# Four PSUM banks for each pool throughout, the first z tile's projection moved ahead, the final norm's sums on TensorE

## The chip, the cores and the metric

The kernel runs on one core of a Trainium2 chip. The metric is the device time of one execution in microseconds. The engines are TensorE (PE, with its weight loads shown as PEld), VectorE (DVE), ScalarE (ACT), GpSimd (POOL) and SyncE (SP), which only issues transfers. TensorE writes to PSUM, of which there are eight banks of 512 float32 values in each of 128 partitions; VectorE and ScalarE read it from there.

## The reference

One layer of an encoder for 384 tokens (128 of running streams, 256 of a new one), all in float32. Cut to what matters:

```
h    = rmsnorm(x, norm1_w);  proj = h @ w_in       # z, x/B/C, dt, u, v
xbc  = silu(causal_conv(x/B/C))
dt   = softplus(dt_raw + dt_bias)
y    = ssd_scan(xs, dt, a, B, C, h0) + d * xs       # 8 groups of 4 heads
y    = group_rmsnorm(y * silu(z))
g    = gelu(u) * spatial_mix(group_rmsnorm(gelu(v)))
x    = x + concat(y, g) @ w_out
h    = rmsnorm(x, norm2_w);  up = causal_conv(h @ w_up)
x    = x + (silu(up[:D_FF]) * up[D_FF:]) @ w_down
out  = x * rsqrt(mean(x * x) + EPS) * final_norm_w
```

The outputs are `out`, the new states of the convolutions and of the scan, and the normalised `v` rows of the running streams.

## The kernel before

Activations lie transposed: 16 tiles `xT` of 128 features by 384 tokens. Every large product is made of three reduced-precision (fp32r) matmuls. Both operands are split into a high part (a cast on ScalarE) and a low part (a subtraction on VectorE): `hh` and `hl` for the normed input, `whi` and `wlo` for a slab of weights. `mm3` (L95 to L97) issues high by high, high by low, low by high. A slab (`slab`, L82) is 128 x 1024 weights; it is loaded by SP into `wraw`, split, and read by 24 matmuls. The pool `wpool` has three buffers for each of `wraw`, `whi` and `wlo`.

`in_proj` (L201) makes one tile of 128 projected features: two slabs, 48 matmuls of 384 columns, in one PSUM bank. The factor 1/rms of a norm is multiplied in afterwards, when VectorE reads the bank.

The order: the first block loads `xT`, sums its squares into `ssum1` and makes the first four tiles of group 0 (`ps_first`) and the `dt` product (`ps_dt`). `rstd_of` (L99) then sums `ssum1` over the partitions with a matmul (L103), takes a root on ScalarE and a reciprocal on VectorE (L111): `r1`. Three transposes of `r1` (L198) give `r1t`, six small records (L255) rearrange `dt`, and a chain of short VectorE instructions makes `dt`, its running sums (L285 to L287) and the decays.

Eight groups of heads follow: `ssd_in(g)` makes the six tiles Bc, Cc, xs0, xs1, zs0, zs1; `ssd(g)` does the scan, with small matmuls between VectorE and ScalarE work (transposes L362 and L371, products L392 to L414, `dk` times `xdt` L456, the new state L488, the group norm L107). The last group's `ssd` is followed by `gmlp(0)`, whose first part `gmlp_v` (L528 to L530) multiplies weights `w_v` as the moving operand, 512 columns, into three banks `pv` at once. Then come three more `gmlp` calls with `w_out` between them, the second norm, and the feed-forward part, `up` and `down`, in eleven chunks. At the end, squares of `xT` are summed into `ssum3` on GpSimd, the last on VectorE; a matmul with one column (L672) sums over partitions; `rt` is the reciprocal root; `rd` is a diagonal of it, and a float32 matmul (L678) spreads it over the partitions; 16 products (L680) give the output.

PSUM is handed out by two pools, `psA` (projections) and `psB` (all else): 3 and 5 banks for the heads. Behind the heads both are closed and opened anew as 4 and 4 (L510 to L512). A tile of a pool waits until a bank of that pool is free. The new pools lie on the banks of the old ones.

The order of each engine's instructions is fixed before the run by a planner: it takes the instruction that is ready in its own timeline and comes first in the program; `tc.high_priority` (the first block and all slabs) moves instructions ahead. On the chip each engine keeps that order.

Of the kernel before, what the change touches and what calls it, by code (L numbers as in the profile page):

```python
# [9 lines left out]
F32 = mybir.dt.float32  # L10
F32R = mybir.dt.float32r
BF16 = mybir.dt.bfloat16
AF = mybir.ActivationFunctionType
ALU = mybir.AluOpType
PSUM = bass.MemoryType.PSUM

P = 128
D = 2048
KT = D // P
NB, LS, LP = 8, 16, 256  # L20
T = NB * LS + LP
NT = T // P
# [15 lines left out]
def encoder_layer(ctx: ExitStack, tc: tile.TileContext, a: dict, o: dict):  # L38
    nc = tc.nc

    def mul(out, x, y, eng=None):
        (eng or nc.vector).tensor_tensor(out=out, in0=x, in1=y, op=ALU.mult)  # L42

    def add(out, x, y, eng=None):
        (eng or nc.vector).tensor_tensor(out=out, in0=x, in1=y, op=ALU.add)  # L45

    def sub(out, x, y, eng=None):
        (eng or nc.vector).tensor_tensor(out=out, in0=x, in1=y, op=ALU.subtract)  # L48
# [4 lines left out]
    def act(out, x, f, **kw):  # L53
        nc.scalar.activation(out=out, in_=x, func=f, **kw)

    const = ctx.enter_context(tc.tile_pool(name="const", bufs=1))
    wpool = ctx.enter_context(tc.tile_pool(name="wpool", bufs=3))
    mixp = ctx.enter_context(tc.tile_pool(name="mixp", bufs=3))
    big = ctx.enter_context(tc.tile_pool(name="big", bufs=1))
    ps_ctx = ExitStack()  # L60
    psA = ps_ctx.enter_context(tc.tile_pool(name="psA", bufs=3, space=PSUM))
    psB = ps_ctx.enter_context(tc.tile_pool(name="psB", bufs=5, space=PSUM))
    dram = ctx.enter_context(tc.tile_pool(name="dram", bufs=1, space=bass.MemoryType.DRAM))

    def ctile(name, shape, src=None, eng=None):
# [6 lines left out]
    xT = [big.tile([P, T], F32, name=f"xT{k}") for k in range(KT)]  # L72
# [26 lines left out]
    def rstd_of(ssum, n, name, pool, parts=None):  # L99

        ps = psB.tile([P, 512], F32, name="psb")
        if parts is None:
            nc.tensor.matmul(ps[:, :T], ones, ssum, start=True, stop=True)  # L103
        else:
            split(ssum, *parts)
            for i, x in enumerate(parts):
                nc.tensor.matmul(ps[:, :T], onesr, x, start=i == 0, stop=i == 1)  # L107
        sq = pool.tile([P, T], F32, name=name + "_q", tag="rsq")
        act(sq, ps[:, :T], AF.Sqrt, bias=eps, scale=1.0 / n)
        r = pool.tile([P, T], F32, name=name, tag="rstd")  # L110
        nc.vector.reciprocal(out=r, in_=sq)  # L111
        return r
# [19 lines left out]
    ssum1 = const.tile([P, T], F32, name="ssum1", tag="ssum")  # L132
    first_ctx = ExitStack()
    fst_p = first_ctx.enter_context(tc.tile_pool(name="first", bufs=1))
    ps_dt = psB.tile([P, 512], F32, name="psb")
    ps_first = [(psB if j == 3 else psA).tile([P, 512], F32, name="psb" if j == 3 else "psa") for j in range(4)]
    with tc.high_priority(offset=AHEAD):
        warm = fst_p.tile([P, 512], BF16, name="warm")
        nc.vector.memset(warm, 0.0)
# [36 lines left out]
        ones = ctile("ones", [P, P], eng=nc.sync)  # L176
        ident = ctile("ident", [P, P], eng=nc.sync)
# [12 lines left out]
    nfw = ctile("final", [P, KT])  # L190
    onesr = const.tile([P, P], F32R, name="onesr")
    nc.vector.tensor_copy(out=onesr, in_=ones)
    r1 = rstd_of(ssum1, D, "r1", const)
    first_ctx.close()
    r1t = const.tile([P, NT], F32, name="r1t")
    psr = psB.tile([P, 512], F32, name="psb")
    for t in range(NT):
        nc.tensor.transpose(out=psr[:, t * P : (t + 1) * P], in_=r1[:, t * P : (t + 1) * P], identity=ident)  # L198
    nc.scalar.copy(out=r1t, in_=psr[:, : NT * P].rearrange("p (t i) -> p t i", t=NT)[:, :, 0])

    def in_proj(src, ps=None):  # L201

        ps = psA.tile([P, 512], F32, name="psa") if ps is None else ps
        for half in range(2):
            hi, lo = slab(src[half])
            for k in range(8):
                kk = half * 8 + k
                mm3(ps[:, :T], w_of((hi, lo), k), (hh[kk], hl[kk]), kk == 0, kk == KT - 1)
        return ps

    def w_out(cs, mixes, done=None):

# [44 lines left out]
    x, e, s, q, p = (m2[:, i * W : (i + 1) * W] for i in range(5))  # L257
# [78 lines left out]
    def ssd_in(g):  # L336
        cst = sp.tile([P, 4, NB + 1, KC - 1], F32, name="cst", bufs=2)
        nc.gpsimd.dma_start(out=cst, in_=a["conv_st"][g])
        nst = sp.tile([P, 4, NB + 1, KC - 1], F32, name="nst", bufs=2)
        h0 = sp.tile([P, NB, 4 * HD], F32, name="h0")  # L340
        nc.gpsimd.dma_start(out=h0, in_=a["h0T"][g])
        res = []
        for j, nm in enumerate(("Bc", "Cc", "xs0", "xs1")):
            ps = ps_first[j] if g == 0 else in_proj(a["w_ssd"][g, j])
            t = sp.tile([P, T], F32, name=nm, bufs=2)
            conv_silu(ps, 4 * g + j, cst, nst, j, t)
            res.append(t)
        nc.gpsimd.dma_start(out=o["nconv"][g], in_=nst)
        for j in range(2):
            ps = in_proj(a["w_ssd"][g, 4 + j], psB.tile([P, 512], F32, name="psb") if g == j == 0 else None)  # L350
            t = sp.tile([P, T], F32, name=f"zs{j}")
            mul(t, ps[:, :T], r1)
            act(t, t, AF.Silu)
            res.append(t)
        return res + [h0]

    def ssd(g, Bc, Cc, xs0, xs1, zs0, zs1, h0):
# [123 lines left out]
        Bh = sp.tile([P, P], F32R, name="Bh")  # L481
        Bl = sp.tile([P, P], F32R, name="Bl")
        split(Bt[:, 0], Bh, Bl)
        pn = [psB.tile([P, 512], F32, name="psb") for _ in range(NB // 2)]
        for i, (w, x) in enumerate(((Bh, xwh), (Bh, xwl), (Bl, xwh))):
            for q in range(NB // 2):
                rows = slice(32 * q, 32 * q + 32)
# [19 lines left out]
            w_out([g // 2 - 1], [mixes[g - 2], mixes[g - 1]])  # L507
        mixes[g] = ssd(g, *ins)
    sp_ctx.close()
    ps_ctx.close()  # L510
    psA = ctx.enter_context(tc.tile_pool(name="psA2", bufs=4, space=PSUM))
    psB = ctx.enter_context(tc.tile_pool(name="psB2", bufs=4, space=PSUM))  # L512


    gp_ctx = ExitStack()
# [139 lines left out]
    yw = []  # L655
    ssum3 = const.tile([P, T], F32, name="ssum3", tag="ssum")
    rt = const.tile([P, NT], F32, name="rt")
    for k in range(KT):
        sq = fp.tile([P, T], F32, name="nsq", bufs=2)
        act(sq, xT[k], AF.Square)  # L660
        if k == 0:
            nc.gpsimd.tensor_copy(out=ssum3, in_=sq)
        else:
            add(ssum3, ssum3, sq, None if k == KT - 1 else nc.gpsimd)
        if k == KT // 2:
            act(rt[:, :1], ssum3[:, :1], AF.Sqrt)
        yw.append(fp.tile([P, T], F32, name=f"yw{k}"))
        act(yw[k], xT[k], AF.Copy, scale=nfw[:, k : k + 1])

    pc = psB.tile([P, 512], F32, name="psb")  # L670
    for t in range(NT):
        nc.tensor.matmul(pc[:, t : t + 1], ssum3[:, t * P : (t + 1) * P], ones[:, :1], start=True, stop=True)  # L672
    act(rt, pc[:, :NT], AF.Sqrt, bias=eps, scale=1.0 / D)
    nc.vector.reciprocal(out=rt, in_=rt)
    rd = fp.tile([P, NT, P], F32, name="rd")
    mul(rd, ident.unsqueeze(1).to_broadcast([P, NT, P]), rt.unsqueeze(2).to_broadcast([P, NT, P]))
    pr = psB.tile([P, 512], F32, name="psb")
    nc.tensor.matmul(pr[:, :T], ones, rd.rearrange("p t i -> p (t i)"), start=True, stop=True)  # L678
    for k in range(KT):
        mul(xT[k], yw[k], pr[:, :T])  # L680
        (nc.scalar if k % 2 else nc.sync).dma_start(out=o["y"][:, k, :], in_=xT[k])
# [129 lines left out]
```

## Time and profile before

| | us |
|---|---|
| median of 3 runs | 2178.97 (2177.57 to 2179.19) |
| profiled execution, its time | 2177.31 |
| profiled execution, its span | 2175.5 |
| TensorE busy | 2135.3 (98%) |
| VectorE busy | 1350.6 (62%) |
| ScalarE busy | 796.9 (37%) |
| GpSimd busy | 226.5 (10%) |

The span runs from the first to the last instruction; the time also holds what lies around it. Starts in the trace are counted from the start of the span. A matmul's row lasts longer than its share of TensorE, since matmuls overlap; what one costs is the distance to the next one's start.

### The profile page before, as it was taken

To read this page: it belongs to the slowest core of one execution; us is meant where nothing else is said; L and a number is where in the kernel's file an instruction comes from. 1 tells how busy PE (TensorE), PEld (TensorE's weight loads), DVE (VectorE), ACT (ScalarE), POOL (GpSimd) and SP (SyncE) were. 2 spreads that over 40 slices of the span, in tenths; PEclk is the share of its full clock that TensorE was granted. 3 is DMA by queue.
4 is the path that set the end of the run, shared out by engine and by line. 5 is a ranking of instruction groups with operands and counts; after the bars stand their busy time and mean duration, and the time that the engine had idled before them with its cause. 6 is when DMAs were issued, how large, how long until landed. Compare 5 with 4: busy or idle time off the path is not lost.

```text
span 2175.5 us, 31214 instructions
## 1 busy us (share of the span) xinstructions
PE 2135.3 (98%) x12313; PEld 2079.3 (96%) x12313; DVE 1350.6 (62%) x2149; ACT 796.9 (37%) x1047; POOL 226.5 (10%) x547
## 2 busy tenths in 40 slices
PE   8999999999979999999999999999999999999997
PEld 8899999999869898989999999999999999999997
DVE  6787786885845454545666565656556565656565
ACT  5554453553533334244432232222222222322224
POOL 1221230320210000000010000000000000000003
PEclk9999999999989999999999999999999999999998
DMA  7344444443434343333333333333333333333332
GB/s 234 110 167 166 154 166 137 164 161 128 154 124 141 132 139 131 126 131 117 129 129 129 128 131 128 132 127 129 128 128 127 128 129 126 129 127 129 128 131 100
DMA packets 86563, 296.59 MB, mean 136 GB/s; under 512 B 10928, under 2 KB 19824, under 8 KB 84368
## 3 DMA queue, kind: packets, MB, share of 16 engines
q1 hardware_dynamic: 78288, 261.20, 35.7%
q0 software_dynamic: 6688, 31.61, 4.4%
q8 instruction: 97, 1.59, 0.3%
q10 hardware_dynamic: 1440, 1.78, 0.2%
q14 instruction: 50, 0.41, 0.1%
HBM read 279.61 MB, written 14.93 MB: 135 GB/s over the span
## 4 chain that ended last, share of the span: by engine, by line
PE 95%; DVE 2%; ACT 0%; issue 0%; DVEq 0%; ACTq 0%
PE psa L97 28%; PE psa L95 28%; PE psa L96 28%; PE psa L528 2%; PE psa L530 2%; PE psa L529 2%; PE psb L456 1%; PE psb L569 0%; DVE xT L42 0%; PE psb L414 0%; PE psb L488 0%; PE psb L461 0%; PE psb L392 0%; PE psb L371 0%; PE psb L460 0%
## 5 line engine op out<-in xcount | busy, mean ns | idle before, releaser
L90 ACT CAST whi<-wraw 128x1024 fp32r<-128x1024 f32 x480 | 504.5, 1051 | 1016.5 <-PE psa L96 644.1
L48 DVE TENSOR_TENSOR wlo<-wraw,whi 128x1024 fp32r<-128x1024 f32 x480 | 586.9, 1223 | 342.0 <-ACT whi L90 338.4
L95 PE MATMUL psa<-hh,whi 128*128 128x384 f32 x2352 | 790.8, 336 | 2.0 <-ACT whi L90 2.0
L97 PE MATMUL psa<-hh,wlo 128*128 128x384 f32 x2352 | 790.2, 336 | 2.5 <-DVE wlo L48 2.5
L96 PE MATMUL psa<-hl,whi 128*128 128x384 f32 x2352 | 789.0, 335 | 0.0
L97 PEld LDWEIGHTS psa<-hh,wlo 128*128 128x128 f32 x2352 | 442.7, 188 | 6.4 <-DVE wlo L48 3.1
L96 PEld LDWEIGHTS psa<-hl,whi 128*128 128x128 f32 x2352 | 442.6, 188 | 6.3 <-issue 6.1
L95 PEld LDWEIGHTS psa<-hh,whi 128*128 128x128 f32 x2352 | 442.8, 188 | 4.6 <-ACT whi L90 2.7
L45 DVE TENSOR_TENSOR xT<-xT,psa 128x384 f32<-128x384 f32 x288 | 159.2, 553 | 188.0 <-PE psa L97 188.0
L97 PE MATMUL psa<-gh,wlo 128*128 128x384 f32 x704 | 235.1, 334 | 0.0
L95 PE MATMUL psa<-gh,whi 128*128 128x384 f32 x704 | 235.1, 334 | 0.0
L96 PE MATMUL psa<-gl,whi 128*128 128x384 f32 x704 | 235.1, 334 | 0.0
L95 PE MATMUL psa<-mh,whi 128*128 128x384 f32 x512 | 171.4, 335 | 0.0
L96 PE MATMUL psa<-ml,whi 128*128 128x384 f32 x512 | 171.3, 334 | 0.0
L97 PE MATMUL psa<-mh,wlo 128*128 128x384 f32 x512 | 171.2, 334 | 0.0
L42 DVE TENSOR_TENSOR fpad<-psa,r 128x128 f32<-128x128 f32 (+1 forms) x176 | 54.8, 354 | 155.4 <-PE psa L97 155.4
L95 PEld LDWEIGHTS psa<-gh,whi 128*128 128x128 f32 x704 | 132.1, 188 | 0.0
L96 PEld LDWEIGHTS psa<-gl,whi 128*128 128x128 f32 x704 | 132.1, 188 | 0.0
L97 PEld LDWEIGHTS psa<-gh,wlo 128*128 128x128 f32 x704 | 132.1, 188 | 0.0
L51 DVE SCALAR_TENSOR_TENSOR facc<-fpad,ffnw,facc 128x400 f32<-128x400 f32 x176 | 111.0, 632 | 2.7
L96 PEld LDWEIGHTS psa<-ml,whi 128*128 128x128 f32 x512 | 96.1, 188 | 0.0
L97 PEld LDWEIGHTS psa<-mh,wlo 128*128 128x128 f32 x512 | 96.1, 188 | 0.0
(218 smaller groups left out, 1819.7 us busy)
## 6 DMA issues: line engine op xcount, KB each, us to landing
wraw<-in_w_up SPq DMA_DIRECT2D x176, 512.0 KB, 3.2
wraw<-in_w_ssd SPq DMA_DIRECT2D x88, 512.0 KB, 3.3
wraw<-in_w_down SPq DMA_DIRECT2D x88, 512.0 KB, 3.2
wraw<-in_w_out SPq DMA_DIRECT2D x64, 512.0 KB, 3.2
wraw<-in_w_v SPq DMA_DIRECT2D x32, 512.0 KB, 3.2
wraw<-in_w_u SPq DMA_DIRECT2D x32, 512.0 KB, 3.2
h<-in_h0T POOLq DMA_DIRECT2D x8, 1024.0 KB, 5.9
out_hs<-h POOLq DMA_DIRECT2D x8, 1024.0 KB, 4.4
```

The source lines that it names most:

```text
L42: (eng or nc.vector).tensor_tensor(out=out, in0=x, in1=y, op=ALU.mult)
L45: (eng or nc.vector).tensor_tensor(out=out, in0=x, in1=y, op=ALU.add)
L48: (eng or nc.vector).tensor_tensor(out=out, in0=x, in1=y, op=ALU.subtract)
L51: nc.vector.scalar_tensor_tensor(out=out, in0=x, scalar=s, in1=y, op0=op0, op1=op1)
L90: nc.scalar.copy(out=hi, in_=src)
L95: nc.tensor.matmul(ps, w[0], x[0], start=first, stop=False)
L96: nc.tensor.matmul(ps, w[0], x[1], start=False, stop=False)
L97: nc.tensor.matmul(ps, w[1], x[0], start=False, stop=last)
L456: nc.tensor.matmul(tt(pd[rows], t), xdt[f][:, t, rows], tt(dk[:, hh_], t), start=True, stop=t == 1)
L528: nc.tensor.matmul(pv[t], hh[kk][:, ts_], hi[:, ws], start=first, stop=False)
L529: nc.tensor.matmul(pv[t], hh[kk][:, ts_], lo[:, ws], start=False, stop=False)
L530: nc.tensor.matmul(pv[t], hl[kk][:, ts_], hi[:, ws], start=False, stop=last)
```

## The change

Both pools have four banks from the start to the end and are not closed. All four of `ps_first` come from `psA`. The projection of the first z tile (`ps_z0`) is called directly behind the sums of the first norm, with a bank of `psB`, ahead of the transposes of `r1`; `ssd_in(0)` uses it. Of the four banks `pn` in `ssd`, one comes from `psA`. In the final norm the first square goes straight into `ssum3`; the last square `sq` is not added to it, but summed by matmuls of its own into the same columns. `rt` is split into a reduced-precision part `rth` and the rest; two diagonals are made, one on VectorE and one on ScalarE, and two reduced-precision matmuls with `onesr` spread them.

```diff
--- before.py
+++ after.py
@@ -57,9 +57,8 @@
     wpool = ctx.enter_context(tc.tile_pool(name="wpool", bufs=3))
     mixp = ctx.enter_context(tc.tile_pool(name="mixp", bufs=3))
     big = ctx.enter_context(tc.tile_pool(name="big", bufs=1))
-    ps_ctx = ExitStack()
-    psA = ps_ctx.enter_context(tc.tile_pool(name="psA", bufs=3, space=PSUM))
-    psB = ps_ctx.enter_context(tc.tile_pool(name="psB", bufs=5, space=PSUM))
+    psA = ctx.enter_context(tc.tile_pool(name="psA", bufs=4, space=PSUM))
+    psB = ctx.enter_context(tc.tile_pool(name="psB", bufs=4, space=PSUM))
     dram = ctx.enter_context(tc.tile_pool(name="dram", bufs=1, space=bass.MemoryType.DRAM))
 
     def ctile(name, shape, src=None, eng=None):
@@ -133,7 +132,7 @@
     first_ctx = ExitStack()
     fst_p = first_ctx.enter_context(tc.tile_pool(name="first", bufs=1))
     ps_dt = psB.tile([P, 512], F32, name="psb")
-    ps_first = [(psB if j == 3 else psA).tile([P, 512], F32, name="psb" if j == 3 else "psa") for j in range(4)]
+    ps_first = [psA.tile([P, 512], F32, name="psa") for _ in range(4)]
     with tc.high_priority(offset=AHEAD):
         warm = fst_p.tile([P, 512], BF16, name="warm")
         nc.vector.memset(warm, 0.0)
@@ -190,14 +189,6 @@
     nfw = ctile("final", [P, KT])
     onesr = const.tile([P, P], F32R, name="onesr")
     nc.vector.tensor_copy(out=onesr, in_=ones)
-    r1 = rstd_of(ssum1, D, "r1", const)
-    first_ctx.close()
-    r1t = const.tile([P, NT], F32, name="r1t")
-    psr = psB.tile([P, 512], F32, name="psb")
-    for t in range(NT):
-        nc.tensor.transpose(out=psr[:, t * P : (t + 1) * P], in_=r1[:, t * P : (t + 1) * P], identity=ident)
-    nc.scalar.copy(out=r1t, in_=psr[:, : NT * P].rearrange("p (t i) -> p t i", t=NT)[:, :, 0])
-
     def in_proj(src, ps=None):
 
         ps = psA.tile([P, 512], F32, name="psa") if ps is None else ps
@@ -207,6 +198,15 @@
                 kk = half * 8 + k
                 mm3(ps[:, :T], w_of((hi, lo), k), (hh[kk], hl[kk]), kk == 0, kk == KT - 1)
         return ps
+
+    r1 = rstd_of(ssum1, D, "r1", const)
+    ps_z0 = in_proj(a["w_ssd"][0, 4], psB.tile([P, 512], F32, name="psb"))
+    first_ctx.close()
+    r1t = const.tile([P, NT], F32, name="r1t")
+    psr = psB.tile([P, 512], F32, name="psb")
+    for t in range(NT):
+        nc.tensor.transpose(out=psr[:, t * P : (t + 1) * P], in_=r1[:, t * P : (t + 1) * P], identity=ident)
+    nc.scalar.copy(out=r1t, in_=psr[:, : NT * P].rearrange("p (t i) -> p t i", t=NT)[:, :, 0])
 
     def w_out(cs, mixes, done=None):
 
@@ -347,7 +347,7 @@
             res.append(t)
         nc.gpsimd.dma_start(out=o["nconv"][g], in_=nst)
         for j in range(2):
-            ps = in_proj(a["w_ssd"][g, 4 + j], psB.tile([P, 512], F32, name="psb") if g == j == 0 else None)
+            ps = ps_z0 if g == j == 0 else in_proj(a["w_ssd"][g, 4 + j])
             t = sp.tile([P, T], F32, name=f"zs{j}")
             mul(t, ps[:, :T], r1)
             act(t, t, AF.Silu)
@@ -481,7 +481,7 @@
         Bh = sp.tile([P, P], F32R, name="Bh")
         Bl = sp.tile([P, P], F32R, name="Bl")
         split(Bt[:, 0], Bh, Bl)
-        pn = [psB.tile([P, 512], F32, name="psb") for _ in range(NB // 2)]
+        pn = [psB.tile([P, 512], F32, name="psb") for _ in range(NB // 2 - 1)] + [psA.tile([P, 512], F32, name="psa")]
         for i, (w, x) in enumerate(((Bh, xwh), (Bh, xwl), (Bl, xwh))):
             for q in range(NB // 2):
                 rows = slice(32 * q, 32 * q + 32)
@@ -507,9 +507,6 @@
             w_out([g // 2 - 1], [mixes[g - 2], mixes[g - 1]])
         mixes[g] = ssd(g, *ins)
     sp_ctx.close()
-    ps_ctx.close()
-    psA = ctx.enter_context(tc.tile_pool(name="psA2", bufs=4, space=PSUM))
-    psB = ctx.enter_context(tc.tile_pool(name="psB2", bufs=4, space=PSUM))
 
 
     gp_ctx = ExitStack()
@@ -655,13 +652,15 @@
     yw = []
     ssum3 = const.tile([P, T], F32, name="ssum3", tag="ssum")
     rt = const.tile([P, NT], F32, name="rt")
+    rth = const.tile([P, NT], F32R, name="rth")
     for k in range(KT):
-        sq = fp.tile([P, T], F32, name="nsq", bufs=2)
-        act(sq, xT[k], AF.Square)
         if k == 0:
-            nc.gpsimd.tensor_copy(out=ssum3, in_=sq)
+            act(ssum3, xT[k], AF.Square)
         else:
-            add(ssum3, ssum3, sq, None if k == KT - 1 else nc.gpsimd)
+            sq = fp.tile([P, T], F32, name="nsq", bufs=2)
+            act(sq, xT[k], AF.Square)
+            if k < KT - 1:
+                add(ssum3, ssum3, sq, nc.gpsimd)
         if k == KT // 2:
             act(rt[:, :1], ssum3[:, :1], AF.Sqrt)
         yw.append(fp.tile([P, T], F32, name=f"yw{k}"))
@@ -669,13 +668,19 @@
 
     pc = psB.tile([P, 512], F32, name="psb")
     for t in range(NT):
-        nc.tensor.matmul(pc[:, t : t + 1], ssum3[:, t * P : (t + 1) * P], ones[:, :1], start=True, stop=True)
+        for x in (ssum3, sq):
+            nc.tensor.matmul(pc[:, t : t + 1], x[:, t * P : (t + 1) * P], ones[:, :1], start=x is ssum3, stop=x is sq)
     act(rt, pc[:, :NT], AF.Sqrt, bias=eps, scale=1.0 / D)
     nc.vector.reciprocal(out=rt, in_=rt)
-    rd = fp.tile([P, NT, P], F32, name="rd")
-    mul(rd, ident.unsqueeze(1).to_broadcast([P, NT, P]), rt.unsqueeze(2).to_broadcast([P, NT, P]))
+    nc.vector.tensor_copy(out=rth, in_=rt)
+    sub(rt, rt, rth.bitcast(F32))
+    rd = [fp.tile([P, NT, P], F32R, name=f"rd{i}") for i in range(2)]
     pr = psB.tile([P, 512], F32, name="psb")
-    nc.tensor.matmul(pr[:, :T], ones, rd.rearrange("p t i -> p (t i)"), start=True, stop=True)
+    for t in range(NT):
+        act(rd[1][:, t], ident, AF.Copy, scale=rt[:, t : t + 1])
+    mul(rd[0], ident.unsqueeze(1).to_broadcast([P, NT, P]), rth.bitcast(F32).unsqueeze(2).to_broadcast([P, NT, P]))
+    for i in range(2):
+        nc.tensor.matmul(pr[:, :T], onesr, rd[i].rearrange("p t i -> p (t i)"), start=i == 0, stop=i == 1)
     for k in range(KT):
         mul(xT[k], yw[k], pr[:, :T])
         (nc.scalar if k % 2 else nc.sync).dma_start(out=o["y"][:, k, :], in_=xT[k])
```

## Rows read from the trace of the kernel before

**Rows 1.** TensorE's waits: who for whom, us in total, times, longest.

```profile
PE psb L456 <- DVE dk L42: 6.2, 1, 6.2
PE psb L198 <- DVE r L111: 3.3, 1, 3.3
PE psa L97 <- DVE wlo L48: 2.5, 2, 1.8
...
PE psa L528 <- ACT gr_q L54: 2.0, 1, 2.0
```

**Rows 2.** Busy time by stretch; the first line names the columns.

```profile
core 0: us, PE busy (x) PEld busy (x) DVE busy (x) ACT busy (x) POOL busy (x), PEclk, DMA share, GB/s
...
51.90:55.88 3.98, 3.98 (x13) 3.97 (x13) 3.52 (x10) 1.65 (x3) 1.04 (x2) 0.51 0.00 0
591.20:616.17 24.97, 9.95 (x63) 6.03 (x62) 17.42 (x33) 6.73 (x11) 6.02 (x10) 0.72 0.15 59
616.17:619.40 3.23, 3.23 (x8) 2.60 (x9) 3.19 (x3) 0.00 (x1) 0.00 (x0) 0.56 0.20 84
100.00:850.00 750.00, 734.97 (x4314) 694.93 (x4313) 503.11 (x804) 319.80 (x430) 120.20 (x202) 0.99 0.44 148
1300.00:2158.00 858.00, 858.00 (x4952) 857.97 (x4950) 505.27 (x777) 259.10 (x300) 62.30 (x218) 1.00 0.38 126
```

**Rows 3.** TensorE in order of time, 45 to 77 us: start, duration, what.

```profile
45.60 0.81 PE L103 MATMUL psb<-ssum,ones 128*128 128x384 f32 x2
49.66 0.90 PE L198 MATMUL psb<-ident,r 128*128 128x128 f32 x3 [3.26 <-DVE r L111]
...
51.91 0.69 PE L95 MATMUL psa<-hh,whi 128*128 128x384 f32 x1
...
73.37 0.30 PE L285 MATMUL psb<-yo,mask 128*128 128x32 f32 x2
...
76.31 0.52 PE L95 MATMUL psb<-hh,whi 128*128 128x384 f32 x1
```

**Rows 4.** ScalarE in order of time, 15 to 60 us.

```profile
20.55 1.04 ACT L90 CAST whi<-wraw 128x1024 fp32r<-128x1024 f32 x1
...
58.12 1.03 ACT L90 CAST whi<-wraw 128x1024 fp32r<-128x1024 f32 x1
```

**Rows 5.** VectorE in order of time, 64 to 72 us.

```profile
70.08 1.25 DVE L305 TENSOR_SCALAR yo<-yo,bmask 128x32 f32<-128x32 f32 x8
```

**Rows 6.** TensorE in order of time, first group of heads, 105 to 107 us.

```profile
105.41 0.66 PE L456 MATMUL psb<-dk,xdt 128*64 128x128 f32 x8
...
106.43 0.49 PE L461 MATMUL psb<-ident,yo 128*128 128x128 f32 x2
```

**Rows 7.** TensorE in order of time, last group of heads, 604 to 617 us.

```profile
605.47 1.12 PE L456 MATMUL psb<-dk,xdt 128*64 128x128 f32 x8 [6.22 <-DVE dk L42]
...
607.38 0.80 PE L461 MATMUL psb<-ident,yo 128*128 128x128 f32 x2
...
616.17 0.80 PE L528 MATMUL psa<-whi,hh 128*128 128x512 f32 x1 [2.01 <-ACT gr_q L54]
```

**Rows 8.** All engines in order of time, 2159 to 2164 us.

```profile
2159.61 0.56 DVE L45 TENSOR_TENSOR ssum<-ssum,nsq 128x384 f32<-128x384 f32 x1 [0.72 <-ACT nsq L54]
...
2160.22 0.83 PE L672 MATMUL psb<-ones,ssum 128*128 128x1 f32 x6 [1.93 <-DVE ssum L45]
...
2161.38 0.18 DVE L674 RECIPROCAL rt<-rt 128x3 f32<-128x3 f32 x1 [1.22 <-ACT rt L54]
2161.59 0.56 DVE L42 TENSOR_TENSOR rd<-ident,rt 128x384 f32<-128x384 f32 x1
...
2162.20 1.65 PE L678 MATMUL psb<-rd,ones 128*128 128x384 f32 x2 [1.16 <-DVE rd L42]
2163.89 0.55 DVE L42 TENSOR_TENSOR xT<-yw,psb 128x384 f32<-128x384 f32 x1 [1.74 <-PE psb L678]
```

**Rows 9.** Groups of ScalarE instructions by shape: busy us, mean ns.

```profile
L90 ACT CAST Bh<-Bt 128x128 fp32r<-128x128 f32 x8 | 2.4, 294 | 0.1
```

## The prediction

> **What bounds the kernel now.** I read the list of TensorE's waits first. It is short: all in it is at three places, the first norm, the last group of heads and the final norm [rows 1]. The windows by stretch say why nothing else is there: from 1300 to 2158 us TensorE is busy in all 858.00 us with 4952 matmuls, 0.1733 us each at clock 1.00 [rows 2]. So the kernel is TensorE's queue plus its holes, and an edit is worth the holes it fills, with the slow clock behind them.
>
> The first hole, from the timeline. The norm's sums end at 45.60 + 0.81 = 46.41; TensorE then stands 3.26 us for the reciprocal `r`, and the matmuls behind it run at clock 0.51 [rows 2, 3]. The next landmark, L285, starts at 73.37. In between lie 72 projection matmuls (`z1` and half of group 1's `Bc`) and the nine small records of L198 and L255. The first z tile is not among them: its matmuls, the ones into `psb`, begin at 76.31 [rows 3]. Its two slabs were split by 20.55 + 1.04 [rows 4] and sit in two of the three slab buffers until then. So everything else goes through the one buffer left: the fourth cast starts at 58.12, when `z1`'s first half is through [rows 4], and TensorE waits for splits again (L97 2.5 us in two waits [rows 1], and L95 a little less).
>
> The second hole, 591.20 to 616.17: busy 9.95 of 24.97 us, so 15.02 idle, at mean clock 0.72 [rows 2]. Group 7 has no next group whose projections could stand in. The longest wait is 6.2 us for VectorE's `dk` [rows 1, 7]. What ends it is telling: the first `w_v` matmul waits 2.01 us for ScalarE's `gr_q` [rows 7], an instruction that has no data for it, but is the last reader of the old PSUM pools. `hh` and `hl` are long there. So the stage behind waits for banks.
>
> The third is the chain from the last sum at 2159.61 to the first output product at 2163.89 [rows 8]. From 73.37 to 590, eight groups with 5 and 3 banks, no wait is listed.
>
> **The change, part by part.** *z0 behind the sums.* 48 matmuls become ready at 46.41 with weights already split, and nothing new is issued ahead of them (the slab loads are on SP and done). They take 48 x 0.1733 = 8.32 us and cover the 3.26 us. L198 and L255 queue behind them, to about 54.7 instead of 49.66. With both slab buffers free from 50.6 and 54.7 on, the fourth and fifth splits run while TensorE has `z1`'s first half, so the later waits lose their cause. Full-speed need of what lies between 46.41 and 73.37: 72 x 0.1733 = 12.48, plus the nine small records, which took 51.91 - 49.66 = 2.25 us at the low clock [rows 3]; between half of that and all of it, I take 1.5. 26.96 - 13.98 = 12.98 us to be had. I take 12.0, leaving 1 us for small waits. Bounds: 13.4 (records at half), and 5.2 if only the first wait and the slow stretch behind it go: 3.26 + (3.98 - 12 x 0.1733 = 1.90) [rows 2, 3].
>
> What is late next: L255 feeds VectorE's chain for `dt`, which ends with L305 at 71.3 [rows 5], and L285 must follow. It starts 5 us later now. Ahead of L285 TensorE has `z1` (to about 64.5) and then group 1's projections; four `psA` banks hold `z1` and three more, 25 us, so the cover reaches 89 us. If that cover were gone, each microsecond of lateness past it would count in full.
>
> *Pools not closed.* `gmlp_v` needs three `psA` banks, slabs, `hh` and `hl`; its `vg` and `gw` still wait for the heads' SBUF pool, but they come behind its 144 matmuls. Those are 512 wide; by 512/384 x 0.1733 = 0.231 us they are 33 us of filling for a hole of 15.0. Gain: 15.0 idle; then the clock. Two heads' products took 607.38 - 605.47 = 1.91 us in group 7 and 106.43 - 105.41 = 1.02 in group 0 [rows 6, 7]; if all 9.95 us were slow, 9.95 x (1 - 1.02/1.91) = 4.6 would come back; I take 4.0. Eight `w_v` matmuls after 616.17 took 3.23 us at clock 0.56, 1.85 at full speed [rows 2]: 1.4. Against it: slabs are now split inside the heads' chain and make `dk` later, but behind filled time; and changes of tile on TensorE, some ten of about 0.15 us, my estimate: 1.4. Sum 19.0; bounds 20.4 and 13 (a third unfilled, when slabs come late).
>
> *Five and three banks become four and four.* For `pn` one bank comes from `psA`, so a group still finds four. That part costs nothing as long as projections of the next group hide it: VectorE is busy 503 of 750 us [rows 2], so a group has a third of its time as slack. Bounds 0 and +3 us; I take +1.
>
> *Final norm.* Removed: the last VectorE sum, 2160.22 - 2159.61 = 0.61 with its hand-over. Added: three more sums on TensorE. Six records took 0.83 us [rows 8], 0.138 each. As the code lists pairs, only the first pair's first half can be ahead of the last square; ten records follow, 1.38: +0.55. If all three first halves ran ahead it is +0. The Trainium skill (PSUM — Partial Sum Buffer, The four PSUM rules) says that two accumulation groups open at once in one bank cannot both start with the clearing matmul, which would forbid running ahead; no row here shows it, and by it the part stands at +0.55. Then the broadcast: before, `rd` 0.56 and a float32 matmul of 1.65 from 2161.59 to 2163.89 = 2.30 [rows 8]. Now a copy and a subtraction of three columns (0.18 each, as the reciprocal [rows 8]), three ScalarE products of 128 columns (0.294 each [rows 9]) beside VectorE's 0.56, and one visible reduced matmul, 0.69 at the low clock as the first of `z1` [rows 3]: 0.36 + 0.88 + 0.69 + 0.1 for hand-overs = 2.03: -0.27. Sum -0.61 + 0.55 - 0.27 = -0.3; bounds -1.2 (halves ahead, products overlapping) and +0.6.
>
> **Sum.** -12.0 - 19.0 + 1.0 - 0.3 = -30.3 us. The profiled execution took 2177.31 us, of which 2175.5 are its span; that gives 2147.0. The median of the runs is 1.66 us higher, so 2148.7 from there. I say 2148.
>
> **The rivals.** (a) *The second hole stays*: `w_v` matmuls are kept behind the heads by something other than banks, such as the order on TensorE or slabs that come too late. For it: the wait names only what came last. Against: earlier groups fill the same chain with projections. 2148 + 19 = 2167.
> (b) *The chain takes the first hole back*: L255 behind z0 makes L285 and all of group 0 late, and TensorE waits there. For it: that chain ends only at 71.3 as it is [rows 5]. Against: 25 us of projections. The gain falls to the 5.2: 2155.
> (c) *Slower*: four `psB` banks starve the heads' chain. Place: the run from `p1` to `rstd_of`, where three `pn` tiles, a `pd` and the norm's sums ask for banks while `psA`, full of the next group's tiles, gives `pn` none. Price: one wait a group, eight in all; it decides from 31.3/8 = 3.9 us each, about half a projection (8.3). At 5 us: 2148 + 40 = 2188. Against: a projection tile is read as soon as it is done.
> (d) *The change does not do what it says*: the planner keeps z0 and `w_v` late. Then 2178.
>
> **How the numbers follow.** Forecast 0.73, (a) 0.09, (b) 0.11, (c) 0.04, (d) 0.03. 0.2%, 4.4 us, is about what can be told from no change. Faster: 0.73 + 0.09 + 0.11 = 0.93; same 0.03; slower 0.04. The range 2140 to 2160 holds the forecast's own (2142 to 2154, from the bounds of its terms) and (b), 0.84 together; (a), (c) and (d) are left out.
>
> **What would show it.** Right: no wait of L198 on `r`; matmuls into `psb` from 46.4 us; L285 no later than before, with at least 48 more projection matmuls done; no L528 on `gr_q`, L528 records between those of group 7's L456 and L107; granted clock 1.00 in both stretches. Wrong: a wait of L285, L456 or L488 of several microseconds in every group, or pieces of the 15 us still idle between 580 and 605.

## The result and the profile after

The changed kernel takes 2195.03 us (median of 4 runs, 2193.49 to 2197.43) against 2179.08 (2177.57 to 2183.56) before: ratio 1.0071, 95% interval 1.0053 to 1.0089. It is slower by 16 us where 2148 was forecast. The profiled execution took 2193.76 us, its span is 2192.0. Lines of the new file in this part: L94 to L96 are `mm3`, L102 the sums of the first norm, L208 the transposes of `r1`, L525 to L527 the `w_v` products.

TensorE's list of waits in the changed kernel answers to [rows 1]; columns as there:

```profile
PE psb L397 <- DVE xwP L42: 17.6, 8, 2.4
PE psb L285 <- DVE yo L51: 7.1, 1, 7.1
PE psa L94 <- ACT hh L54: 2.7, 1, 2.7
...
PE psb L672 <- ACT nsq L54: 0.5, 1, 0.5
```

All the waits that were to go are gone: `r`, `gr_q`, `wlo`, and the 6.2 us for `dk`. In their place stand one at L397, 0.8 us in group 0 and 2.4 us in each of the seven others, and 7.1 us at L285. In the kernel before, L397 was waited for once, in the last group (at 593.60), which has no next group's projections to stand in:

```profile
PE psb L397 <- DVE xwP L42: 2.4, 1, 2.4
```

So the changed kernel has in nearly every group what the kernel before has in its last one.

TensorE in order of time in the changed kernel, 48 to 87 us, which answers to [rows 3]:

```profile
48.30 0.81 PE L102 MATMUL psb<-ssum,ones 128*128 128x384 f32 x2
48.65 0.63 PE L94 MATMUL psb<-hh,whi 128*128 128x384 f32 x1
...
57.26 0.49 PE L208 MATMUL psb<-ident,r 128*128 128x128 f32 x3
57.68 0.85 PE L255 MATMUL psb<-sel,dk 64*128 64x32 f32 x6
58.46 0.44 PE L94 MATMUL psa<-hh,whi 128*128 128x384 f32 x1
...
66.72 0.34 PE L96 MATMUL psa<-hh,wlo 128*128 128x384 f32 x1
74.18 0.63 PE L285 MATMUL psb<-yo,mask 128*128 128x32 f32 x2 [7.12 <-DVE yo L51]
...
85.85 0.49 PE L488 MATMUL psa<-xwh,Bh 32*128 32x512 f32 x1
86.27 0.44 PE L94 MATMUL psa<-hh,whi 128*128 128x384 f32 x1
```

The z tile runs behind the sums as planned (the matmuls into `psb`, 48.65 to 57.26), then `z1`. But at 66.9 projections stop, although group 1's `Bc` should follow. None runs for 19 us, and the next one stands directly behind a single L488 whose output is `psa`: the `pn` tile that now comes from `psA`. The same in group 1:

```profile
141.64 0.49 PE L362 MATMUL psb<-ident,Bc 128*128 128x128 f32 x3
...
142.62 0.83 PE L392 MATMUL psb<-Cc,Bc 128*128 128x128 f32 x6
145.86 0.67 PE L397 MATMUL psb<-xwP,Bt 128*128 128x256 f32 x2 [2.40 <-DVE xwP L42]
...
147.88 0.49 PE L488 MATMUL psa<-xwh,Bh 32*128 32x512 f32 x1
148.30 0.44 PE L94 MATMUL psa<-hh,whi 128*128 128x384 f32 x1
```

Between L392 and L397 no projection stands; before, 34 stood there in each of the groups 1 to 6. The windows of the changed kernel, columns as in [rows 2]:

```profile
67.00:85.85 18.85, 10.95 (x48) 7.88 (x48) 12.74 (x47) 8.35 (x18) 3.12 (x5) 0.64 0.25 88
...
100.00:850.00 750.00, 733.20 (x4248) 690.72 (x4247) 491.35 (x797) 297.40 (x412) 107.61 (x201) 0.99 0.43 145
...
1300.00:2158.00 858.00, 858.00 (x4952) 858.00 (x4951) 510.10 (x788) 251.58 (x285) 54.15 (x215) 1.00 0.38 128
```

From 1300 us on nothing changed (4952 matmuls in 858 us both times). Between 100 and 850 us TensorE issued 66 matmuls fewer than in [rows 2].

The whole span can be cut at three landmarks that every version has: the row with the last of group 1's three L362, the same row of group 7 (in some versions one of its three transposes runs ahead of the other two), and the start of the 144th `w_v` matmul. Between the first two, the changed kernel and the one before issue the same work (2767 and 2769 matmuls by the windows). Each row is one execution. In us, and in brackets the difference to before:

| kernel | start to group 1 | six groups | group 7 to `w_v` done | the rest | span |
|---|---|---|---|---|---|
| before | 138.90 | 450.60 | 60.57 | 1525.43 | 2175.5 |
| changed | 141.64 (+2.7) | 478.30 (+27.7) | 47.70 (-12.9) | 1524.36 (-1.1) | 2192.0 (+16.5) |

So the second hole paid 12.9 us, the first one nothing, and six groups of heads cost 27.7 us, 4.6 each. The experiments ask what takes these 4.6 us, and what ate the first hole. The table is continued at their end.

### The profile page after: what moved, and what is told of

It reads as the page before. It is cut to its first block, busy times and chain, and to the rows that moved or that the text cites. A ratio compares the mean times of both kernels' runs of the same rounds, so it can differ in the third digit from the quotient of the medians.

```text
span 2192.0 us, 31165 instructions
## 1 busy us (share of the span) xinstructions
PE 2149.8 (98%) x12319; PEld 2088.5 (95%) x12319; DVE 1345.1 (61%) x2150; ACT 777.9 (35%) x1036; POOL 216.6 (10%) x546
## 4 chain that ended last, share of the span: by engine, by line
PE 97%; DVE 2%; issue 0%; DMA 0%; ACT 0%; DVEq 0%; ACTq 0%
PE psa L94 29%; PE psa L95 29%; PE psa L96 29%; PE psa L525 2%; PE psa L527 2%; PE psa L526 2%; PE psb L456 1%; PE psb L566 0%; DVE wlo L48 0%; PE psa L488 0%; PE psb L414 0%; PE psb L488 0%; DVE xT L42 0%; PE psb L461 0%; DVE xwP L42 0%
## 5 line engine op out<-in xcount | busy, mean ns | idle before, releaser
L94 PE MATMUL psa<-hh,whi 128*128 128x384 f32 x2352 | 790.2, 336 | 0.0
L96 PE MATMUL psa<-hh,wlo 128*128 128x384 f32 x2352 | 789.1, 335 | 0.0
L94 PEld LDWEIGHTS psa<-hh,whi 128*128 128x128 f32 x2352 | 442.9, 188 | 3.5 <-issue 3.2
L96 PEld LDWEIGHTS psa<-hh,wlo 128*128 128x128 f32 x2352 | 442.9, 188 | 1.1 <-issue 1.1
L96 PE MATMUL psa<-gh,wlo 128*128 128x384 f32 x704 | 235.1, 334 | 0.0
L94 PE MATMUL psa<-gh,whi 128*128 128x384 f32 x704 | 235.1, 334 | 0.0
L94 PE MATMUL psa<-mh,whi 128*128 128x384 f32 x512 | 171.4, 335 | 0.0
L96 PE MATMUL psa<-mh,wlo 128*128 128x384 f32 x512 | 171.2, 334 | 0.0
L94 PEld LDWEIGHTS psa<-gh,whi 128*128 128x128 f32 x704 | 132.1, 188 | 0.0
L96 PEld LDWEIGHTS psa<-gh,wlo 128*128 128x128 f32 x704 | 132.1, 188 | 0.0
L96 PEld LDWEIGHTS psa<-mh,wlo 128*128 128x128 f32 x512 | 96.1, 188 | 0.0
```

Of the source, the lines that this page charges most:

```text
L94: nc.tensor.matmul(ps, w[0], x[0], start=first, stop=False)
L96: nc.tensor.matmul(ps, w[1], x[0], start=False, stop=last)
```

## The experiments

Two theories. *The order of the banks*: a pool hands out its banks in the order of the program. The `pn` tile of group g stands, in the program, ahead of the projections of later tiles; once it comes from `psA`, no projection behind it gets a bank, and so none is queued, until that tile has its own first matmul, which needs the end of VectorE's chain. *The number of banks*: rival (c), four `psB` banks are too few for the chain. In the expectations P is the first theory, and the other letters are ways to blame something else.

**One: all four `pn` from `psB`**, on the changed kernel; 4 and 4 banks stay.

```diff
-        pn = [psB.tile([P, 512], F32, name="psb") for _ in range(NB // 2 - 1)] + [psA.tile([P, 512], F32, name="psa")]
+        pn = [psB.tile([P, 512], F32, name="psb") for _ in range(NB // 2)]
```

> The changed kernel with all four pn tiles taken from psB again, all else as changed. Theory P (a pool gives out its banks in the order of the program, so the pn tile in psA stands ahead of all later psA tiles and no projection of the next group can be queued before that tile's first matmul): the projections come back between L392 and L397 in every group. The changed kernel lost 4.6 us in each of six groups, some 12 us in group 0 and some 4 in the last, so 2195 - 44 = about 2151 us, with no wait of L397 on xwP. Theory Q (four psB banks are too few for the heads' chain): the four pn tiles now want all of psB, so it stays above 2188 us, waits of L397 included.

Measured: 2155.0 us (2154.25 to 2155.61), ratio 0.9886 (0.9871 to 0.9901). L397 and L285 have left the list of waits. That one line turns 16 us of loss into 24 of gain, with as few `psB` banks as before and one more tile to take from them. Group 1 again, TensorE in order of time:

```profile
129.67 0.82 PE L371 MATMUL psb<-ident,xs 128*128 128x128 f32 x6
130.24 0.42 PE L94 MATMUL psa<-hh,whi 128*128 128x384 f32 x1
...
138.85 0.34 PE L94 MATMUL psa<-hh,whi 128*128 128x384 f32 x1
139.02 0.59 PE L397 MATMUL psb<-xwP,Bt 128*128 128x256 f32 x2
```

Projections stand ahead of L397 and cover the chain.

**Two: that line alone**, on the kernel before, with its 3 and 5 banks: the same edit the other way round.

```diff
-        pn = [psB.tile([P, 512], F32, name="psb") for _ in range(NB // 2)]
+        pn = [psB.tile([P, 512], F32, name="psb") for _ in range(NB // 2 - 1)] + [psA.tile([P, 512], F32, name="psa")]
```

> The kernel before with one edit: the fourth pn tile comes from psA (three and five banks, pools closed as before). Theory P: the same loss without any of the rest, 4.6 us in seven groups and more in group 0: about 2179 + 32 = 2211 us, L397 waiting 2.4 us on xwP in each group. Theory Q: psB has five banks and one user less, so no loss: 2179 us within 4.

Measured: 2219.5 us (2210.84 to 2221.37), ratio 1.0169 (1.0144 to 1.0193). Its list of TensorE's waits begins:

```profile
PE psb L397 <- DVE xwP L42: 19.2, 8, 2.4
PE psb L456 <- DVE dk L42: 4.0, 1, 4.0
...
PE psb L285 <- DVE yo L51: 2.7, 1, 2.7
```

Five `psB` banks, three `pn` tiles taken from them, so more room than before, and the same wait of 2.4 us in each group. So the number of `psB` banks is not the cause of this wait. The time lies 8 us above what theory P expected, and part of that is the clock: over the six groups between the landmarks the mean granted clock is 0.97, 0.99 in the changed kernel. The four runs spread over 10 us, and the fastest has the highest clock over the whole run (0.987, the others 0.982 to 0.984).

**Three: the z tile's slabs later.** In the changed kernel the first norm's sums start 2.70 us later than in [rows 3], at 48.30. `in_proj` is called early, and its slabs have `AHEAD`'s priority. SP's first issue and ScalarE's first long work are now theirs; two views in order of time, of SP and of ScalarE:

```profile
0.76 0.39 SPq L84 DMA_DIRECT2D wraw<-in_w_ssd  x1
```

```profile
4.88 1.04 ACT L89 CAST whi<-wraw 128x1024 fp32r<-128x1024 f32 x1 [1.92 <-DMA wraw<-in_w_ssd]
```

```diff
-    def slab(src):
-        with tc.high_priority(offset=AHEAD):
+    def slab(src, ahead=AHEAD):
+        with tc.high_priority(offset=ahead):
...
-    ps_z0 = in_proj(a["w_ssd"][0, 4], psB.tile([P, 512], F32, name="psb"))
+    ps_z0 = in_proj(a["w_ssd"][0, 4], psB.tile([P, 512], F32, name="psb"), AHEAD - 150)
```

> The changed kernel with the two slabs of z0 moved ahead by 150 places less, so that their loads and splits come behind the first loads of the first block. Theory S (the z0 call moved its slab loads and splits to the very front of SP, ScalarE and VectorE, and delayed the first block by 2.7 us): the norm's sums start at 45.6 instead of 48.3 us, total 2195 - 2.7 = 2192 us. Rival: the 2.7 us are a matter of the run, or the later wait for L285 eats them: 2195 us.

Measured: 2192.19 us (2189.43 to 2198.89), ratio 1.0061 (1.0041 to 1.0082). The sums start at 46.9, 1.4 us earlier than in the changed kernel; the waits of L397 (17.4 us) and L285 (7.1) stay. The size, some 3 us, is as expected, but the runs of the two kernels overlap, and the trace shows 1.4 us of the 2.7. The rest need not come from the slabs: in experiments two and eight, whose edits touch nothing ahead of the first norm, the sums start at 47.15 and 45.52.

**Four: one and three together.**

> Both edits of the two runs before on the changed kernel: pn from psB, z0's slabs 150 places later. Theories P and S together: 2151 - 2.7 = about 2148 us, which is what was forecast for the change. If Q holds: above 2186 us.

Measured: 2152.62 us (2151.69 to 2153.08), ratio 0.9875 (0.986 to 0.9889): 2.4 us better than experiment one, and here the runs do not overlap (the spans of the two profiled executions differ by 1.54 us, all of it ahead of group 1). From the sums (46.85) to the final norm TensorE's list has no wait at all. Still, 2148 was expected: 4 us are missing with no idle time to show for them.

**Five: a bank of its own for the fourth `pn`.** `psA` has three banks, a pool `psC` one, `psB` four. This tells order from number once more: `pn` is not among the projections' tiles, and `psB` is as small as in the changed kernel.

```diff
-    psA = ctx.enter_context(tc.tile_pool(name="psA", bufs=4, space=PSUM))
+    psA = ctx.enter_context(tc.tile_pool(name="psA", bufs=3, space=PSUM))
+    psC = ctx.enter_context(tc.tile_pool(name="psC", bufs=1, space=PSUM))
...
-    ps_first = [psA.tile([P, 512], F32, name="psa") for _ in range(4)]
+    ps_first = [(psC if j == 3 else psA).tile([P, 512], F32, name="psc" if j == 3 else "psa") for j in range(4)]
...
-        pn = [psB.tile([P, 512], F32, name="psb") for _ in range(NB // 2 - 1)] + [psA.tile([P, 512], F32, name="psa")]
+        pn = [psB.tile([P, 512], F32, name="psb") for _ in range(NB // 2 - 1)] + [psC.tile([P, 512], F32, name="psc")]
```

> The changed kernel with psA at three banks and a pool of its own, of one bank, for the fourth pn tile (and for the fourth of the first tiles). psB stays at four. Theory P (the order in which psA gives out its banks): pn no longer stands in that order, so the time falls to that of the kernel with pn in psB, 2155 us within 4, though no bank is added. Theory R (what hurts is that pn takes a bank away from the projections and holds it over the heads' chain): the projections still have three banks, so it stays near 2195 us.

Measured: 2158.38 us (2157.74 to 2158.89), ratio 0.99 (0.9886 to 0.9913). No wait of L397, and a time near P's, although `psA` has a bank less for projections; theory R is refuted. One new wait, behind `w_v`: its three `pv` tiles hold all of `psA`, and the first projection that follows waits until `vg`'s instruction has read one, 2.50 us at 632.16.

**Six: only the pools**, on the kernel before: 4 and 4 throughout, not closed, `pn` from `psB`, all of `ps_first` from `psA`; z tile and final norm as before.

```diff
-    psA = ps_ctx.enter_context(tc.tile_pool(name="psA", bufs=3, space=PSUM))
-    psB = ps_ctx.enter_context(tc.tile_pool(name="psB", bufs=5, space=PSUM))
+    psA = ctx.enter_context(tc.tile_pool(name="psA", bufs=4, space=PSUM))
+    psB = ctx.enter_context(tc.tile_pool(name="psB", bufs=4, space=PSUM))
...
-    ps_ctx.close()
-    psA = ctx.enter_context(tc.tile_pool(name="psA2", bufs=4, space=PSUM))
-    psB = ctx.enter_context(tc.tile_pool(name="psB2", bufs=4, space=PSUM))
```

> The kernel before with the pools alone: four and four banks from start to end, not closed; pn stays in psB, no z0 ahead, final norm as before. The last group's hole was 15.0 us idle plus slow clock, forecast at 19.0; the kernel with pn in psB and slabs later gained 26.4 in all. If the forecast of this hole holds: 2179 - 19 = 2160 us, no wait of L528 on gr_q. If the products between the heads' records cost what the clock gives back: 2179 - 15 = 2164 us. If four psB banks cost anything in the groups, waits of L397 or L488 show and it is slower than that.

Measured: 2166.38 us (2165.89 to 2168.83), ratio 0.9941 (0.9925 to 0.9956). The window of the last group is filled:

```profile
580.00:640.00 60.00, 60.00 (x325) 50.50 (x325) 39.78 (x61) 22.93 (x31) 8.06 (x13) 1.00 0.38 127
```

The stretch from group 7 to the end of `w_v` takes 41.91 us in place of 60.57: -18.7. But the six groups ahead of it cost 6.6 us more than before. The expectation had four `psB` banks cost something only together with waits of L397 or L488; here they cost without one.

**Seven: only the z tile ahead**, on the kernel before, slabs 150 places later, its 3 and 5 banks and the closing as they were. `in_proj` stands ahead of it, as in the change.

```diff
     r1 = rstd_of(ssum1, D, "r1", const)
+    ps_z0 = in_proj(a["w_ssd"][0, 4], psB.tile([P, 512], F32, name="psb"), AHEAD - 150)
...
-            ps = in_proj(a["w_ssd"][g, 4 + j], psB.tile([P, 512], F32, name="psb") if g == j == 0 else None)
+            ps = ps_z0 if g == j == 0 else in_proj(a["w_ssd"][g, 4 + j])
```

> The kernel before with z0's projection behind the first norm's sums alone (slabs 150 places later, pools of three and five, closed as before). Forecast for this hole: 12.0 us, so 2167 us. The rest of the 26.4 us if the other hole is worth 15 to 19: 7 to 11, so 2168 to 2172 us. If the chain of dt takes the hole back: a wait of L285 and 2174 us or more.

Measured: 2164.62 us (2164.03 to 2166.67), ratio 0.993 (0.9917 to 0.9944). Group 1 begins at 126.83: -12.1 us. The six groups take 450.24, as before, and the last group's hole is still there (60.39). No wait of L285.

**Eight: only the final norm**, on the kernel before: the last two hunks of the change, as they stand.

```diff
-        nc.tensor.matmul(pc[:, t : t + 1], ssum3[:, t * P : (t + 1) * P], ones[:, :1], start=True, stop=True)
+        for x in (ssum3, sq):
+            nc.tensor.matmul(pc[:, t : t + 1], x[:, t * P : (t + 1) * P], ones[:, :1], start=x is ssum3, stop=x is sq)
...
-    nc.tensor.matmul(pr[:, :T], ones, rd.rearrange("p t i -> p (t i)"), start=True, stop=True)
+    for i in range(2):
+        nc.tensor.matmul(pr[:, :T], onesr, rd[i].rearrange("p t i -> p (t i)"), start=i == 0, stop=i == 1)
```

> The kernel before with the final norm alone changed. From the last sum of xT to the first output product the changed kernel took 5.21 us against 5.56, so 2179 - 0.35 = 2178.6 us, which a timing will not tell from 2179; by the trace the stretch should again be 5.2 us.

Measured: 2178.37 us (2175.97 to 2180.98, 11 runs) against 2180.43 (15 runs), ratio 0.9993 (0.9984 to 1.0002). The expected tenths of a microsecond lie inside the interval; from the runs alone this part is not told from nothing. In the trace the stretch is 5.21 us (2158.79 to 2164.00), as expected.

**Nine and ten: three and five banks, never closed, against four and four.** Where are the silent 6.6 us of six and the missing 4 of four? Nine is experiment four with `psA` at 3 and `psB` at 5 banks; ten is experiment four again, on the same chip.

```diff
-    psA = ctx.enter_context(tc.tile_pool(name="psA", bufs=4, space=PSUM))
-    psB = ctx.enter_context(tc.tile_pool(name="psB", bufs=4, space=PSUM))
+    psA = ctx.enter_context(tc.tile_pool(name="psA", bufs=3, space=PSUM))
+    psB = ctx.enter_context(tc.tile_pool(name="psB", bufs=5, space=PSUM))
...
-    ps_first = [psA.tile([P, 512], F32, name="psa") for _ in range(4)]
+    ps_first = [(psB if j == 3 else psA).tile([P, 512], F32, name="psb" if j == 3 else "psa") for j in range(4)]
```

> The changed kernel with psA of 3 and psB of 5 banks all through, all four pn and ps_first's fourth tile from psB, z0's slabs at a priority 150 places later, new final norm. If four psB banks in place of five are what cost about 5 us over the six middle groups (more and dearer small records without a wait), they cost nothing here: 2179 - 13 (first hole) - 18.7 (second hole) - 0.4 (final norm) + 2.5 (w_v waits once for a third psA bank, as with the pool of pn's own) = 2149 to 2150, and the six groups take 444 to 448 us. If that cost comes from something else that goes with pools that aren't closed, or with z0 ahead, the six groups stay at 455 to 458 us and the time is 2155 to 2157.

> The changed kernel with all four pn from psB and z0's slabs 150 places later, again, on the same chip as the kernel with three and five banks, so that the two are told apart by 3 us or less: 2152.6 as before, six groups at 455 to 456 us.

Measured: nine 2149.03 us (2148.77 to 2149.17), ratio 0.9862 (0.9845 to 0.9878); ten 2152.57 (2151.98 to 2152.92), ratio 0.9878 (0.9863 to 0.9892). The six groups, between the marks of the table, take 450.34 us in nine and 457.00 in ten (449.0 and 455.7 from L397 to L397, as the expectation counts; 1 us above its 444 to 448). So the silent cost goes with the four `psB` banks. Where it lies shows in group 2, TensorE in order of time, first nine (3 and 5):

```profile
240.96 0.51 PE L488 MATMUL psb<-xwh,Bh 32*128 32x512 f32 x4
241.29 0.40 PE L488 MATMUL psb<-xwl,Bh 32*128 32x512 f32 x4
241.53 0.40 PE L488 MATMUL psb<-xwh,Bl 32*128 32x512 f32 x4
241.86 0.44 PE L96 MATMUL psa<-hh,wlo 128*128 128x384 f32 x1
```

then ten (4 and 4):

```profile
243.24 0.51 PE L488 MATMUL psb<-xwh,Bh 32*128 32x512 f32 x3
243.57 0.40 PE L488 MATMUL psb<-xwl,Bh 32*128 32x512 f32 x3
243.81 0.40 PE L488 MATMUL psb<-xwh,Bl 32*128 32x512 f32 x3
244.14 0.45 PE L96 MATMUL psa<-hh,wlo 128*128 128x384 f32 x1
...
247.02 0.34 PE L94 MATMUL psa<-hh,whi 128*128 128x384 f32 x1
247.29 0.49 PE L488 MATMUL psb<-xwh,Bh 32*128 32x512 f32 x1
247.63 0.39 PE L488 MATMUL psb<-xwl,Bh 32*128 32x512 f32 x1
247.86 0.39 PE L488 MATMUL psb<-xwh,Bl 32*128 32x512 f32 x1
248.18 0.44 PE L95 MATMUL psa<-hl,whi 128*128 128x384 f32 x1
248.46 0.34 PE L96 MATMUL psa<-hh,wlo 128*128 128x384 f32 x1
```

Twelve matmuls of 32 rows take 0.90 us (240.96 to 241.86), nine of them 0.90, and three 0.89 (247.29 to 248.18). With four banks the fourth `pn` tile gets none in time, its three matmuls follow alone, and cost as much again as all twelve. That is 0.89 us a group. The second batch also breaks the row of projections once more: the one ahead of it and the one behind it take 0.27 and 0.28 us to the next start (247.02 to 247.29, 248.18 to 248.46) in place of the usual 0.173, 0.2 us more together. For six groups 1.09 us each make 6.5 of the 6.66 us between nine and ten. TensorE is busy all the time, so no list of waits shows it; the number of records does (48 L488 rows in ten, 24 in nine, for 96 matmuls in both).

The table of landmarks, continued:

| kernel | start to group 1 | six groups | group 7 to `w_v` done | the rest |
|---|---|---|---|---|
| one | 129.34 (-9.6) | 457.00 (+6.4) | 41.89 (-18.7) | -1.5 |
| two | 149.42 (+10.5) | 484.20 (+33.6) | 60.08 (-0.5) | +0.5 |
| five | 130.84 (-8.1) | 456.74 (+6.1) | 41.70 (-18.9) | +2.1 |
| six | 139.72 (+0.8) | 457.23 (+6.6) | 41.91 (-18.7) | -0.3 |
| nine | 126.53 (-12.4) | 450.34 (-0.3) | 40.73 (-19.8) | +4.0 |
| ten | 127.68 (-11.2) | 457.00 (+6.4) | 41.88 (-18.7) | -1.3 |

Experiment eight, which changes nothing ahead of the final norm, has 137.30, 450.71 and 62.52 in the first three columns. So between two executions of the same code the first and the third differ by 1.6 and 2.0 us, the second by 0.1.

Nine's +4.0 is mostly one wait, 3.18 us of L94 on `vg` at 621.17, as in five: the price of a fourth `psA` bank that is missing behind `w_v`, paid once, against 1.1 us in every group. Nine is the fastest version seen, 30 us under the kernel before.

## Why the prediction was wrong

**The step that failed** is the third part of the change: "For `pn` one bank comes from `psA`, so a group still finds four. That part costs nothing as long as projections of the next group hide it". It counts banks and forgets the order in which a pool gives them out. It also rests on a cover which the edit itself takes away: the next group's projections are in the same pool, behind the `pn` tile. In numbers, six groups cost 27.7 us where +1 (at most +3) was put down. 6.4 of it goes with four `psB` banks (experiment ten, same pools without the wait), and 21.3 with the order of the banks (478.30 - 457.00): 6 x 2.4 = 14.4 us idle, and 6.9 more. Windows of the changed kernel, the whole six groups first, then two stretches within them:

```profile
141.64:619.94 478.30, 463.90 (x2767) 440.70 (x2766) 340.47 (x576) 190.84 (x264) 83.20 (x157) 0.99 0.42 144
...
304.52:311.35 6.83, 6.83 (x24) 5.05 (x17) 2.78 (x6) 1.15 (x1) 5.32 (x9) 0.50 0.05 19
464.95:471.78 6.83, 6.83 (x23) 4.92 (x16) 2.85 (x6) 1.21 (x1) 5.24 (x9) 0.50 0.05 20
```

and TensorE in order of time inside the first of them:

```profile
307.39 0.52 PE L96 MATMUL psa<-hh,wlo 128*128 128x384 f32 x1
307.71 0.52 PE L94 MATMUL psa<-hh,whi 128*128 128x384 f32 x1
```

Behind the pause of groups 3 and 5 (TensorE idle for 2.40 us) the granted clock fell to 0.50, the lower of the two levels seen; behind the same pause of groups 1, 2, 4 and 6 it stayed at 1.00. Why it fell in these two and not in the others no run shows. At 0.50 the next projection starts 0.32 us later (307.39 to 307.71), not 0.173, so of 13.66 us some 6.3 are lost. That is an estimate from these rows, and with it all but 0.6 of the 27.7 us is accounted for.

**The bank term itself was mis-sized** also without the wait. Experiments six and ten measure 6.4 to 6.6 us for six groups; if the 1.15 us that ten takes longer than nine in each of the two stretches beside them belong to it too, it is 9.0 for eight. The row for it was in the trace before, where L488 came four at a time too:

```profile
106.85 0.51 PE L488 MATMUL psb<-xwh,Bh 32*128 32x512 f32 x4
```

What was not asked is what a batch of fewer costs. VectorE's slack, from which the term was argued, does not bear on it: TensorE pays, and it has none.

**z0 behind the sums, -12.0.** The term was right by itself: -12.1 in seven and -12.4 in nine, in a stretch in which experiment eight, with the same code, is 1.6 us shorter than the kernel before. In the changed kernel it was taken back in group 0. "Ahead of L285 TensorE has `z1` and then group 1's projections; four `psA` banks hold `z1` and three more" failed by the same order of banks: they held `z1`, and the three others had to wait for `pn`. The text said what it would cost if that cover were gone; it was, 7.1 us of it as idle time at L285. And "nothing new is issued ahead of them" was wrong: the two slabs moved to the head of SP's and ScalarE's queues, and the sums began 2.7 us late. When the slabs were put later, the sums moved by 1.4 to 1.6 us (48.30 to 46.90 in three, 48.40 to 46.85 from one to four), and the medians by 2.8 and 2.4.

**The pools not closed, -19.0.** Right: -18.7 in one, six and ten, though experiment eight, with the same code here, differs from the kernel before by 2.0 us in this stretch. (The 0.15 us that it puts down for a change of tile came from no row; breaking the row of projections costs 0.1 us each way in the rows of ten.) In the changed kernel 12.9 were left, because group 7 too waits at L397 (2.4 us), the granted clock is 0.93 from there to the end of `w_v`, and the `w_v` matmuls can start only behind the lone `pn` (627.64 us, behind an L488 with output `psa` at 626.92).

**The final norm, -0.3.** Right as far as it can be seen. The rows that answer to [rows 8], all engines in order of time in the changed kernel:

```profile
2176.20 0.38 PE L672 MATMUL psb<-ones,ssum 128*128 128x1 f32 x2 [0.34 <-POOL ssum L45]
...
2177.12 0.38 PE L672 MATMUL psb<-ones,nsq 128*128 128x1 f32 x2 [0.55 <-ACT nsq L54]
2177.37 0.36 PE L672 MATMUL psb<-ones,ssum 128*128 128x1 f32 x2
...
2179.83 1.24 PE L683 MATMUL psb<-rd,onesr 128*128 128x384 f32 x2 [1.43 <-DVE rd L42]
2181.11 3.34 DVE L42 TENSOR_TENSOR xT<-yw,psb 128x384 f32<-128x384 f32 x7 [1.33 <-PE psb L683]
```

From the last sum into `xT` (2175.90; before 2158.33) to the first output product there are 5.21 us, 5.56 before: -0.35. Its two halves fit less well: up to the root on ScalarE (2161.09 before, 2178.44 here) it is -0.2, behind it -0.1, where -0.06 and -0.27 had been put down. That the total is met so closely is partly luck. The sums run in the code's order of pairs, so one half only ran ahead of the last square, which was the assumption. The rule quoted from the Trainium skill (PSUM — Partial Sum Buffer, The four PSUM rules) asks for that order as well; since the code has it anyway, this trace does not test the rule.

Against the forecast the terms make 26.7 (six groups), 14.7 (the first hole), 6.1 (the second) and -0.8 (the rest), together 46.7 us of the 47 by which it was missed.

**The rivals.** The sign was (c)'s, and its price (3.9 us a group and more) was near the 4.6 measured, by chance, since the cause is another. Its phrase "while `psA`, full of the next group's tiles, gives `pn` none" has it reversed: `pn`'s place in `psA` gives the next group none. Its mechanism, waits because `psB` has too few banks, is refuted by one and two; what four `psB` banks do cost, 1.1 us a group, comes without a wait. (a) did not happen, as six shows. (b) did, in group 0, for another reason than a long chain: seven and nine have the same chain and no wait. What was named as the sign of error, "a wait of L285, L456 or L488 of several microseconds in every group", came at L285 once, and at L397 in every group, with 2.4 us in seven of the eight.

Not settled: the stretch up to group 1 in experiment two (+10.5 us). By the windows TensorE is idle there for 3.2 us longer than before (13.70 against 10.46), and the mean granted clock is 0.92 in place of 0.96, over a stretch of 149 us; what the rest consists of no run tells.

## What to carry to other kernels

Before moving a tile from one pool to another, write down the pool's requests in the order of the program, and look what stands behind the moved one: if that is the work which hides the chain that the moved tile waits for, the move can cost a pause in every round. Here it did so with four `psA` banks (the changed kernel) as with three (experiment two). A list of waits without an entry isn't a proof that a step is free: small matmuls that run together can fall apart into two batches, and only the count of records shows it. When a call is moved forward, look also at what it issues under a priority of its own.

## What the runs showed of the hardware

Matmuls with 32 rows each, on four different row groups of TensorE, run side by side: a set of four with 512 columns takes 0.33 us to the start of the next set (240.96 to 241.29), and a single one 0.34 (247.29 to 247.63).

The Trainium skill (TensorE: Matmul & The Clock Gate, Part 3: Packing small matmuls — row/col tiling) says that such matmuls overlap in the array and gives 3.07 times as its speedup for four. Here twelve in sets of four take 0.90 us where three alone take 0.89, which is 4 times the work in the same time; for this kernel the measurement decides. So a set that lacks one bank, and is issued as three and one, pays for two sets.
